# A row softmax with relative-position bias on one core: a gated second load, earlier scales, and counts ahead of two loops

## The chip, the core and the metric

The kernel runs on one core of a Trainium2 chip. The core has compute engines that run their own instruction streams: VectorE (DVE in the profile) and ScalarE (ACT) do the arithmetic here, GpSimd (POOL) only makes two small index tables, and SyncE (SP) does nothing but issue loads. Data moves between the chip's main memory (HBM) and the core's working memory through 16 DMA engines that serve several queues; here loads are issued by SP (queue q1) and stores by ScalarE (queue q10). Engines are ordered against each other by semaphores alone: an instruction can wait until a semaphore has a value and add to another when it ends.

The metric is the device time of one execution in microseconds (us), the median of several runs.

## The reference

```python
def reference(logits, rel_bias):          # logits (2, 8, 2112, 2112), rel_bias (8, 33), f32
    max_rel = 16
    pos = np.arange(S)
    rel = pos[:, None] - pos[None, :]
    rel_clipped = np.clip(rel, -max_rel, max_rel) + max_rel
    bias = rel_bias[:, rel_clipped].copy()
    logits = logits + bias[None, :, :, :]
    logits = logits - logits.max(axis=-1, keepdims=True)
    exp = np.exp(logits)
    return (exp / exp.sum(axis=-1, keepdims=True)).astype(np.float32)
```

There are 2 x 8 x 2112 = 33,792 rows of 2112 numbers. Each row gets a bias that depends only on the distance between row and column, clipped to 16 either way, and then a softmax. Input and output are 285.5 MB each.

## The kernel before

**Tiling.** Each of the 128 partitions owns 264 consecutive rows (`RP`) of one head. A chunk is 6 rows (`R`) of every partition, 128 x 6 x 2112 numbers, 6336 KB; it fills one of four buffers `X[0]` to `X[3]` (`NBUF`). Four chunks, 24 rows a partition (`G`), make one turn of the loops, and there are 11 turns (`K`), so 44 chunks.

**The bias.** Along a row the bias is a constant, then a band of 33 values around the diagonal, then a constant; from one row to the next it shifts by one column. At the start VectorE builds one long strip `F` of it in PSUM for all rows that a partition owns. That needs `rel_bias`, which ScalarE loads (line 120) into `F2` after VectorE has cleared the place (line 118). VectorE meanwhile makes small masks (lines 130 to 140), waits for the load (line 141), spreads the table over the partitions (line 142) and fills the strip (lines 145 to 167). At the start of each turn `window(k)` copies the 2135 columns (`SW`) that the next 24 rows need from `F` to `F2` (line 170), and `settle` waits until the copy has ended.

**The three loops.** They are written out by hand; no planner reorders them.

- SP issues the first four loads at once (lines 95 and 96). Then, for each later chunk, it waits until the store of the same buffer has landed (`st[m]`) and issues the load (lines 97 to 100).
- VectorE, for each chunk: `add(m)` waits for the load (`ld[m]`, line 181) and runs six instructions (line 184), one a row, each of which adds the bias, negates and takes the minimum over the row. `scale(m)` waits until all six exps are done (`expd`, line 207), takes six reciprocals of the sums in one instruction (line 208), announces them (`inv`) and scales rows 0 to 3 (line 211).
- ScalarE, for each chunk: `exps(m)` runs one exp a row, with the sum of the row as a by-product, as soon as that row's add is done (lines 190 to 198). `scale_rest(m)` scales rows 4 and 5 once `inv` says so (line 216). `store(k, m)` waits for six scaled rows (`scaled`, line 92) and issues the store (line 93).

`take(eng, sem, n)` (line 86) waits for a semaphore to reach n and takes n off it again; every wait of this kind has line 86 in the profile. `scales_begin` (line 200) is the wait on `inv` that both engines share.

Of the kernel before, what the change touches and what calls it, by code (L numbers as in the profile page):

```python
# [15 lines left out]
def kernel(  # L16
# [6 lines left out]
    nc = tc.nc  # L23
# [5 lines left out]
    RP = B * H * S // P  # L29
# [4 lines left out]
    NBUF = 4  # L34
    R = 6
    G = NBUF * R
    K = RP // G
    assert K * G == RP
    SW = S + G - 1
    DV = 4  # L40

    io = ctx.enter_context(tc.tile_pool(name="io", bufs=1))
    X = [io.tile([P, R * S], FP32, tag=f"X{b}", name=f"X{b}") for b in range(NBUF)]
    F2 = io.tile([P, SW + 1], FP32, tag="F2", name="F2")
# [4 lines left out]
    tot = io.tile([P, NBUF * R], FP32, tag="tot", name="tot")  # L49
    rec = io.tile([P, NBUF * R], FP32, tag="rec", name="rec")  # L50
    num = rec[:, 0 : NB + 1]
    ps = ctx.enter_context(tc.tile_pool(name="ps", bufs=1, space=bass.MemoryType.PSUM))
    F = ps.tile([P, 2560], FP32, tag="F", name="F")
# [11 lines left out]
    def view(t, offset, dims):  # L65
        return bass.AP(tensor=t.tensor, offset=t.offset + offset, ap=[[list(t.ap[0])[0], P]] + dims)

    def rows(t, k, m):
        return bass.AP(
            tensor=t.tensor, offset=t.offset + m * R * S + k * (G * S), ap=[[RP * S, P], [1, R * S]],  # L70
        )

    with tc.tile_critical(no_gpsimd_drain=True):  # L73
# [3 lines left out]
        expd = nc.alloc_semaphore("expd")  # L77
        scaled = nc.alloc_semaphore("scaled")
        inv = nc.alloc_semaphore("inv")
        rb = nc.alloc_semaphore("rb")  # L80
        zero = nc.alloc_semaphore("zero")
        idx = nc.alloc_semaphore("idx")
# [2 lines left out]
        def take(eng, sem, n):  # L85
            eng.wait_ge(sem, n).then_inc(sem, -n)  # L86

        def load(k, m):
            nc.sync.dma_start(out=X[m][:, :], in_=rows(logits, k, m)).then_inc(ld[m], 16)
# [2 lines left out]
            take(nc.scalar, scaled, R)  # L92
            nc.scalar.dma_start(out=rows(out, k, m), in_=X[m][:, :]).then_inc(st[m], 16)

        for m in range(NBUF):
            load(0, m)
        with nc.Fori(0, K - 1, 1, engines=[ENG.SP]) as k:
            for m in range(NBUF):
# [5 lines left out]
        v = nc.vector  # L104
        done = [0]

        def then(ins):
            done[0] += 1
            ins.then_inc(dve, 1)

        def settle():
            take(v, dve, done[0])
            done[0] = 0

        Q = 32
        step = list(F2.ap[0])[0]
        T = F2[:, 0 : H * W]
# [2 lines left out]
        nc.scalar.dma_start(  # L120
            out=bass.AP(tensor=F2.tensor, offset=F2.offset, ap=[[Q * step, P // Q], [1, H * W]]),
            in_=bass.AP(tensor=rel_bias.tensor, offset=rel_bias.offset, ap=[[0, P // Q], [1, H * W]]),
        ).then_inc(rb, 16)
        nc.gpsimd.iota(pid[:, :], pattern=[[0, 2]], base=0, channel_multiplier=1).then_inc(idx, 1)
        nc.gpsimd.iota(
            num, pattern=[[1, NB + 1]], base=0, channel_multiplier=0,
# [11 lines left out]
        for o, n, s, op in ((eq, NB, q, ALU.is_equal), (lt, NB, q, ALU.is_lt), (hsel, NB, h, ALU.is_equal),  # L138
                            (le, NB + 1, q, ALU.is_le), (gt, NB + 1, q, ALU.is_gt)):
            then(v.tensor_scalar(out=o, in0=num[:, 0:n], scalar1=s, scalar2=None, op0=op))  # L140
        v.wait_ge(rb, 16)
        then(v.stream_shuffle(out=T, in_=T, mask=[0] * Q))  # L142
        settle()
# [19 lines left out]
                           in_=view(reg, 1, [[1, NB - 1], [0, RP - W]])))  # L163
# [3 lines left out]
        settle()  # L167

        def window(k):
            then(v.tensor_copy(out=F2[:, 0:SW], in_=F[:, bass.ds(RP - G - k * G, SW)]))  # L170
            settle()

        def row(m, i):
            return X[m][:, i * S : (i + 1) * S]

        def col(t, m, i, n=1):
            c = m * R + i
            return t[:, c : c + n]
# [21 lines left out]
        def scales_begin(eng, m):  # L200
            if m < NBUF - 1:
                eng.wait_ge(inv, m + 1)
            else:
                take(eng, inv, NBUF)

        def scale(m):
            take(v, expd, R)
            v.reciprocal(out=col(rec, m, 0, R), in_=col(tot, m, 0, R)).then_inc(inv, 1 if m < NBUF - 1 else NBUF + 1)  # L208
            scales_begin(v, m)
            for i in range(DV):  # L210
                v.tensor_scalar_mul(out=row(m, i), in0=row(m, i), scalar1=col(rec, m, i)).then_inc(scaled, 1)  # L211

        def scale_rest(m):
            scales_begin(nc.scalar, m)
            for i in range(DV, R):
                nc.scalar.activation(  # L216
                    out=row(m, i), in_=row(m, i), func=ACTF.Copy, scale=col(rec, m, i),
                ).then_inc(scaled, 1)

        with nc.Fori(0, K, 1, engines=[ENG.DVE]) as k:  # L220
            window(k)
            for m in range(NBUF):
                add(m)
                scale(m)
        with nc.Fori(0, K, 1, engines=[ENG.Activation]) as k:
            for m in range(NBUF):
                exps(m)
                scale_rest(m)
                store(k, m)
# [31 lines left out]
```

## Time and profile before

| | |
|---|---|
| three runs | 1325.72, 1326.83 (the median), 1335.42 us |
| the profiled execution, its time | 1327.36 us |
| the profiled execution, its span | 1325.6 us |
| VectorE busy | 866.1 us |
| ScalarE busy | 757.2 us |
| bytes moved | 570.98 MB, mean 431 GB/s |
| 44 loads, 6336 KB each, issue to landing (median) | 39.0 us |
| 44 stores, 6336 KB each, issue to landing (median) | 58.8 us |

The span runs from the first to the last recorded instruction or transfer; the device time has a little around it. Busy times leave out instructions that only wait, branch or issue a DMA; their engine is then written DVEq, ACTq or SPq. In a group's row, the first pair of numbers is the busy time of the group in us and the mean of one in ns, and behind the second bar stands the time for which the engine sat idle just before these instructions, with what ended it. In a window's row come the stretch, its length, then for DVE, ACT and POOL the busy time and the instructions that started in it, the granted TensorE clock, the DMA engines' mean share and GB/s.

### The profile page before, as it was taken

What the parts mean: (1) busy time and instruction counts of PE and PEld (TensorE: products, weight loads), DVE (VectorE), ACT (ScalarE), POOL (GpSimd) and SP (SyncE); (2) the same over time, 40 slices, a digit from 0 to 9 for tenths busy, and PEclk for the clock granted to TensorE, in tenths of its full rate; (3) what the DMA queues carried; (4) which work ended last, traced back from release to release, by engine and by line L of the source; (5) the groups of instructions that cost most, each with busy time, mean ns of one, the idle gap of its engine ahead of it and who ended that gap; (6) DMA issues with size and microseconds to landing.
All of it is one profiled execution on the core that took longest, in us unless ns stands there. A gap on an engine that the chain in (4) does not pass through costs nothing. (4 is left out here: it accounts for less than half of the span.)

```text
span 1325.6 us, 2109 instructions
## 1 busy us (share of the span) xinstructions
DVE 866.1 (65%) x781; ACT 757.2 (57%) x627; POOL 0.4 (0%) x6
## 2 busy tenths in 40 slices
DVE  6886656566766675566667566556766676566663
ACT  3776555556665565555556565555665665555563
POOL 0000000000000000000000000000000000000000
DMA  9999999999999999999999999999999999999998
GB/s 416 416 433 424 441 428 428 441 424 433 441 428 431 436 425 433 439 430 434 434 430 433 437 434 425 437 434 434 428 439 436 422 441 434 431 431 436 428 433 389
DMA packets 12682, 570.98 MB, mean 431 GB/s; under 512 B 1412, under 2 KB 1416, under 8 KB 1416
## 3 DMA queue, kind: packets, MB, share of 16 engines
q1 hardware_dynamic: 6336, 285.48, 50.1%
q10 hardware_dynamic: 6344, 285.48, 49.8%
q14 instruction: 2, 0.02, 0.0%
HBM read 285.48 MB, written 285.47 MB: 431 GB/s over the span
## 5 line engine op out<-in xcount | busy, mean ns | idle before, releaser
L195 ACT ACTIVATE X<-X,nmax 128x2112 f32<-128x2112 f32 x264 | 542.6, 2055 | 508.0 <-DVE nmax L184 475.3
L184 DVE CUSTOM_DVE_ANT_0 X<-X,F 128x2112 f32<-128x2112 f32 x264 | 605.2, 2354 | 322.3 <-DVEq L86 322.3
L211 DVE TENSOR_SCALAR X<-X,rec 128x2112 f32<-128x2112 f32 x176 | 220.3, 1315 | 2.8
L216 ACT ACTIVATE X<-X,rec 128x2112 f32<-128x2112 f32 x88 | 176.1, 2048 | 17.2 <-DVE rec L208 12.2
L208 DVE RECIPROCAL rec<-tot 128x6 f32<-128x6 f32 x44 | 8.4, 191 | 106.2 <-DVEq L86 106.2
L195 ACT ACTIVATION_READ_ACCUMULATOR X<-X,nmax 128x1 f32 x264 | 49.2, 186 | 0.0
L195 ACT ACT_TABLE_LOAD x11 | 14.1, 1283 | 22.6 <-ACTq L86 19.9
L170 DVE COPY F<-F 128x2135 f32 x11 | 26.1, 2373 | 0.5 <-DVEq L86 0.5
L184 DVE DVE_READ_ACCUMULATOR2_ANT nmax<- 128x1 f32 x264 | 21.7, 82 | 0.0
L142 DVE LOAD_MASK_SELECT F<-F x1 | 0.0, 14 | 6.0 <-DMA F<-in_rel_bias_dram 6.0
L162 DVE COPY F<-own 128x1617 f32<-128x1617 f32 x1 | 1.8, 1835 | 0.0
L118 DVE MEMSET F<- 128x264 f32 x1 | 0.3, 278 | 1.1 <-SPq L73 1.1
L140 DVE TENSOR_SCALAR Z<-rec,Z 128x8 f32<-128x8 f32 (+1 forms) x5 | 0.8, 227 | 0.1
L148 DVE TENSOR_REDUCE own<-F 128x33 f32<-128x264 f32 x1 | 0.6, 608 | 0.1
L161 DVE TENSOR_TENSOR F<-F,own 128x264 f32<-128x264 f32 x1 | 0.4, 442 | 0.1
L145 DVE TENSOR_TENSOR F<-F,Z 128x264 f32<-128x264 f32 x1 | 0.4, 428 | 0.1
L142 DVE STREAM_SHUFFLE F<-F 128x264 f32<-128x264 f32 x1 | 0.4, 443 | 0.0
L158 DVE TENSOR_TENSOR F<-Z,own 128x264 f32<-128x264 f32 x1 | 0.4, 432 | 0.0
L166 DVE COPY F<-own 128x247 f32<-128x247 f32 x1 | 0.4, 410 | 0.0
L164 DVE COPY F<-own 128x247 f32<-128x247 f32 x1 | 0.4, 408 | 0.0
L156 DVE SCALAR_TENSOR_TENSOR own<-Z,own 128x8 f32<-128x8 f32 x1 | 0.2, 227 | 0.2 <-DVEq L86 0.2
L153 DVE TENSOR_SCALAR own<-Z,own 128x8 f32<-128x8 f32 x1 | 0.2, 226 | 0.1
(11 smaller groups left out, 1.6 us busy)
## 6 DMA issues: line engine op xcount, KB each, us to landing
X<-in_logits_dram SPq DMA_DIRECT2D x44, 6336.0 KB, 39.0
out_dram<-X ACTq DMA_DIRECT2D x44, 6336.0 KB, 58.8
F<-in_rel_bias_dram ACTq DMA_DIRECT2D x1, 4.1 KB
```

Source lines behind the costliest of these rows:

```text
L140: then(v.tensor_scalar(out=o, in0=num[:, 0:n], scalar1=s, scalar2=None, op0=op))
L142: then(v.stream_shuffle(out=T, in_=T, mask=[0] * Q))
L145: then(v.tensor_tensor(out=heads, in0=view(F2, 0, [[W, H], [1, W]]), in1=view(hsel, 0, [[1, H], [0, W]]), op=ALU.mult))
L148: then(v.tensor_reduce(out=rbK, in_=view(F2, H * W, [[1, W], [W, H]]), axis=mybir.AxisListType.X, op=ALU.add))
L158: then(v.tensor_tensor(out=bands, in0=view(eq, 0, [[1, NB], [0, W]]), in1=view(rbK, W - 1, [[0, NB], [-1, W]]), op=ALU.mult))
L162: then(v.tensor_copy(out=view(F, C0 + W, [[RP, NB - 1], [1, RP - W]]), in_=view(reg, 1, [[1, NB - 1], [0, RP - W]])))
L170: then(v.tensor_copy(out=F2[:, 0:SW], in_=F[:, bass.ds(RP - G - k * G, SW)]))
L184: v.tensor_tensor_reduce(out=row(m, i), in0=row(m, i), in1=F2[:, x : x + S], scale=-1.0, scalar=BIG, op0=ALU.add, op1=ALU.min, accum_out=c ...
L195: nc.scalar.activation(out=row(m, i), in_=row(m, i), func=ACTF.Exp, scale=-1.0, bias=col(nmax, m, i), accum_out=col(tot, m, i),).then_inc( ...
L208: v.reciprocal(out=col(rec, m, 0, R), in_=col(tot, m, 0, R)).then_inc(inv, 1 if m < NBUF - 1 else NBUF + 1)
L211: v.tensor_scalar_mul(out=row(m, i), in0=row(m, i), scalar1=col(rec, m, i)).then_inc(scaled, 1)
L216: nc.scalar.activation(out=row(m, i), in_=row(m, i), func=ACTF.Copy, scale=col(rec, m, i),).then_inc(scaled, 1)
```

## The change

Three things change.

- **The gate.** SP issues the load of the first chunk and then waits for a new semaphore `go`; the loads of chunks 2, 3 and 4 of the first turn follow after it. VectorE's `window(k)` copies the strip in two parts, 1100 columns (`C1`) and the remaining 1035, with a `settle` after each, and adds one to `go` between them. SP waits for it once only.
- **The scales.** `scale(m)` waits for four exps (`A`), takes four reciprocals, announces them and scales rows 0 to 2 (`D`) on VectorE; it then waits for the other two exps, takes their reciprocals, and scales rows 4 and 5. ScalarE scales row 3 alone. Before, VectorE had rows 0 to 3 and ScalarE rows 4 and 5.
- **The counts.** VectorE, after its masks and ahead of its wait for `rel_bias`, adds 1 to a semaphore 32 times and takes the 32 off again; ScalarE does the same 48 times after it has issued the load of `rel_bias`, ahead of its loop.

```diff
-    DV = 4
+    A, D = 4, 3
+    C1 = 1100
...
-        for m in range(NBUF):
+        load(0, 0)
+        nc.sync.wait_ge(go, 1)
+        for m in range(1, NBUF):
             load(0, m)
...
+        def fill(eng, sem, n):
+            for _ in range(n):
+                eng.sem_inc(sem, 1)
+            take(eng, sem, n)
...
+        fill(nc.scalar, padA, 48)
         nc.gpsimd.iota(pid[:, :], pattern=[[0, 2]], base=0, channel_multiplier=1).then_inc(idx, 1)
...
+        fill(v, padV, 32)
         v.wait_ge(rb, 16)
...
         def window(k):
-            then(v.tensor_copy(out=F2[:, 0:SW], in_=F[:, bass.ds(RP - G - k * G, SW)]))
+            x = RP - G - k * G
+            then(v.tensor_copy(out=F2[:, 0:C1], in_=F[:, bass.ds(x, C1)]))
+            settle()
+            v.sem_inc(go, 1)
+            then(v.tensor_copy(out=F2[:, C1:SW], in_=F[:, bass.ds(x + C1, SW - C1)]))
             settle()
...
         def scale(m):
-            take(v, expd, R)
-            v.reciprocal(out=col(rec, m, 0, R), in_=col(tot, m, 0, R)).then_inc(inv, 1 if m < NBUF - 1 else NBUF + 1)
+            def scales(first, stop):
+                for i in range(first, stop):
+                    v.tensor_scalar_mul(out=row(m, i), in0=row(m, i), scalar1=col(rec, m, i)).then_inc(scaled, 1)
+
+            take(v, expd, A)
+            v.reciprocal(out=col(rec, m, 0, A), in_=col(tot, m, 0, A)).then_inc(inv, 1 if m < NBUF - 1 else NBUF + 1)
             scales_begin(v, m)
-            for i in range(DV):
-                v.tensor_scalar_mul(out=row(m, i), in0=row(m, i), scalar1=col(rec, m, i)).then_inc(scaled, 1)
+            scales(0, D)
+            take(v, expd, R - A)
+            v.reciprocal(out=col(rec, m, A, R - A), in_=col(tot, m, A, R - A)).then_inc(invB, 1)
+            take(v, invB, 1)
+            scales(A, R)
 
         def scale_rest(m):
             scales_begin(nc.scalar, m)
-            for i in range(DV, R):
+            for i in range(D, A):
                 nc.scalar.activation(
```

More of the change, by code (lines that the diff above doesn't have):

```diff
@@ L79 @@
         inv = nc.alloc_semaphore("inv")
+        go = nc.alloc_semaphore("go")
+        padV = nc.alloc_semaphore("padV")
+        padA = nc.alloc_semaphore("padA")
+        invB = nc.alloc_semaphore("invB")
         rb = nc.alloc_semaphore("rb")
```

## The prediction

> **What bounds the kernel now.** I read the page from the top: busy shares of the engines first, then the 40 slices, then the DMA queues.
>
> ```profile
> span 1325.6 us, 2109 instructions
> DVE 866.1 (65%) x781; ACT 757.2 (57%) x627; POOL 0.4 (0%) x6
> DMA  9999999999999999999999999999999999999998
> DMA packets 12682, 570.98 MB, mean 431 GB/s; under 512 B 1412, under 2 KB 1416, under 8 KB 1416
> q1 hardware_dynamic: 6336, 285.48, 50.1%
> q10 hardware_dynamic: 6344, 285.48, 49.8%
> L184 DVE CUSTOM_DVE_ANT_0 X<-X,F 128x2112 f32<-128x2112 f32 x264 | 605.2, 2354 | 322.3 <-DVEq L86 322.3
> ```
>
> No compute engine is near full: VectorE idles a third of the span, 322.3 us of it at the wait for a load (line 86 called from `add`). The 16 DMA engines are at nine tenths or more in every slice but the last, and the load queue q1 and the store queue q10 together claim 50.1% + 49.8% = 99.9% of 16 engines' span. The kernel is a transfer of 570.98 MB with the arithmetic beside it. So the next view is the one that gives the rate by stretch, with the two ends finely cut. A row of X is 6 x 2112 x 4 = 50,688 bytes a partition; a DMA moves 128 of these, 8 for each of 16 engines. The window view counts a packet where it starts, so short windows show rounds of packets.
>
> ```profile
> 0.00:1.90 1.90, 0.59 (x4) 0.00 (x0) 0.43 (x6) 1.00 0.00 0
> 1.90:2.50 0.60, 0.52 (x4) 0.00 (x0) 0.00 (x0) 1.00 4.27 1352
> 17.00:17.60 0.60, 0.60 (x1) 0.00 (x0) 0.00 (x0) 1.00 0.00 0
> 17.60:18.20 0.60, 0.13 (x1) 0.00 (x0) 0.00 (x0) 1.00 3.13 1352
> 0.00:33.00 33.00, 22.87 (x35) 12.46 (x12) 0.43 (x6) 1.00 0.98 415
> 33.00:66.00 33.00, 28.66 (x27) 24.76 (x21) 0.00 (x0) 1.00 1.01 421
> 66.00:132.00 66.00, 49.99 (x45) 46.31 (x40) 0.00 (x0) 1.00 0.99 430
> 132.00:264.00 132.00, 82.63 (x73) 72.33 (x59) 0.00 (x0) 1.00 1.00 430
> 264.00:528.00 264.00, 175.22 (x155) 154.57 (x128) 0.00 (x0) 1.00 1.00 433
> 1056.00:1320.00 264.00, 164.53 (x147) 146.66 (x122) 0.00 (x0) 1.00 1.00 433
> 1322.00:1322.50 0.50, 0.00 (x0) 0.00 (x0) 0.00 (x0) 1.00 0.24 101
> 1322.50:1326.00 3.50, 0.00 (x0) 0.00 (x0) 0.00 (x0) 1.00 0.00 0
> ```
>
> The last two columns are the DMA share and GB/s. In 17.60:18.20, 1352 GB/s x 0.6 us = 811 KB, 16 packets: all 16 engines start their ninth packet, the first of chunk 2. Each costs 3.13 x 0.6 x 16 / 16 = 1.88 us. In 1.90:2.50 the very first 16 packets cost 4.27 x 0.6 = 2.56 us each, 0.68 more, because the engines start from rest. From 264 us on the rate is 433 GB/s and does not move.
>
> The span adds up from this alone: 570.98 MB / 433 GB/s = 1318.6 us; the slower rows lose 33 x (1 - 415/433) = 1.4, 33 x (1 - 421/433) = 0.9, 66 x 3/433 = 0.5 and 132 x 3/433 = 0.9, together 3.7; no packet starts after 1322.5, so some 3.3 us follow the last start. That is 1325.6. Only the 3.7 and the ends can be gained; only a hole in the DMA work can be lost.
>
> **The change, part by part.** *The scales.* Rows of chunk 1, from the timeline (start, duration):
>
> ```profile
> 27.90 2.06 ACT L195 ACTIVATE X<-X,nmax 128x2112 f32<-128x2112 f32 x1
> 32.35 0.08 DVE L184 DVE_READ_ACCUMULATOR2_ANT nmax<- 128x1 f32 x1
> 32.56 2.05 ACT L195 ACTIVATE X<-X,nmax 128x2112 f32<-128x2112 f32 x1 [0.23 <-ACTq L86]
> 34.85 0.19 DVE L208 RECIPROCAL rec<-tot 128x6 f32<-128x6 f32 x1 [2.43 <-DVEq L86]
> 35.08 5.01 DVE L211 TENSOR_SCALAR X<-X,rec 128x2112 f32<-128x2112 f32 x4
> 40.34 0.38 ACTq L93 DMA_DIRECT2D out_dram<-X  x1
> ```
>
> Today VectorE waits 2.43 us after its last add for the sixth exp, takes 0.23 to the first scale, and does four scales of 5.01/4 = 1.25. After: the fourth exp (27.90 + 2.06, and its accumulator read) is done near 30.2, before the adds end at 32.43, so that wait disappears. 32.43 + 0.1 + 0.23 = 32.76; three scales to 36.5; the sixth exp has long ended (34.8), a second reciprocal of 0.23; two scales to 39.2. ScalarE's one scale, 2.0 from 34.8, ends at 36.8. The store is issued near 39.4 instead of 40.34: 0.9 us sooner in each of 44 chunks. Is that on the path? The store then stands behind others:
>
> ```profile
> L93 ACTq DMA_DIRECT2D out_dram<-X x44: 338/338/380, 40.3 to 1306.3; - x44
> DMA to landing us min/median/max: 18.2/58.8/59.5
> 1303.00:1306.30 3.30, 3.05 (x3) 2.01 (x2) 0.00 (x0) 1.00 1.10 476
> 1306.30:1307.30 1.00, 0.00 (x0) 0.00 (x0) 0.00 (x0) 1.00 0.47 203
> 1307.30:1309.10 1.80, 0.00 (x0) 0.00 (x0) 0.00 (x0) 1.00 1.04 451
> ```
>
> A store takes 58.8 us (median) to land, though alone it lands in 18.2; some 40 us of queue and sharing cover it. Even the last one: around its issue at 1306.3 the engines are still moving the store before, 3.30 x 1.10 + 0.47 + 1.80 x 1.04 = 5.97 of 6.1 us. I cost the whole part at nothing; if the cover were gone, it would be worth 0.9 us at the end, once.
>
> *The counts.* 32 increments on VectorE and 48 on ScalarE, each set followed by a wait that resets it. Nothing like a bare increment loop is in the trace; the nearest rows are the wait-and-reset pairs and, from above, the hop between two dependent vector instructions.
>
> ```profile
> L86 DVEq EVENT_SEMAPHORE  x118: 21/21/21, 1.6 to 1300.9; - x118
> 9.33 0.43 DVE L145 TENSOR_TENSOR F<-F,Z 128x264 f32<-128x264 f32 x1
> 9.90 0.61 DVE L148 TENSOR_REDUCE own<-F 128x33 f32<-128x264 f32 x1
> 8.74 0.01 DVE L142 LOAD_MASK_SELECT F<-F  x1 [5.99 <-DMA F<-in_rel_bias_dram]
> 21.07 2.05 ACT L195 ACTIVATE X<-X,nmax 128x2112 f32<-128x2112 f32 x1 [17.10 <-DVE nmax L184]
> ```
>
> Lower end 0.021 us each, upper end 9.90 - 9.76 = 0.14. I take 0.06. VectorE: 32 x 0.06 = 1.9, at most 4.5, inside the 5.99 us in which it waits for rel_bias; it is uncovered only above 5.99/32 = 0.19 each. ScalarE: at most 48 x 0.14 = 6.7, inside 17.10. Cost nothing.
>
> *The gate.* SP (SyncE) issues chunk 1's load as before, then waits for `go`; behind that wait stand the loads of chunks 2 to 4 and SP's whole loop. `go` comes from VectorE when 1100 columns of the strip are copied.
>
> ```profile
> 12.38 1.83 DVE L162 COPY F<-own 128x1617 f32<-128x1617 f32 x1
> 14.44 0.41 DVE L166 COPY F<-own 128x247 f32<-128x247 f32 x1
> 15.35 2.38 DVE L170 COPY F<-F 128x2135 f32 x1 [0.50 <-DVEq L86]
> 18.66 2.36 DVE L184 CUSTOM_DVE_ANT_0 X<-X,F 128x2112 f32<-128x2112 f32 x1 [0.94 <-DVEq L86]
> 0.97 2.02 SPq L89 DMA_DIRECT2D X<-in_logits_dram  x4
> ```
>
> Copies cost (1.83 - 0.41)/(1617 - 247) = 1.04 ns a column and 0.15 us fixed, so 1100 columns take 1.30: 15.35 + 1.30 = 16.65. The hop 0.14, the increment 0.06 and SP's wake, about 0.1 (an estimate, between 0.02 and 0.14 as above): SP issues at about 16.95. From SP's first issue at 0.97 to the first packets at 1.90 to 2.50 passed 0.93 to 1.53, so chunk 2's packets start at 17.88 to 18.48, where before they started at 17.60 to 18.20: a hole of 0.3 us on all engines. Starting from rest, they may again pay the 0.68 of the first round. Sum +1.0. Ends: below, 0.0, if issuing is a little quicker and nothing starts from rest; above, the first part as dear as the whole copy (2.38), +1.1, so 2.1. I take 1.0, nearest to the one start from rest that the trace has.
>
> On the start, the Trainium skill (DMA: Bandwidth & Descriptors, section Latency and other measured facts) gives about 600 ns to the first byte for DMAs issued from SP; this trace shows 0.93 or more. By the page's figure the packets would come at 17.55, before the engines run dry, and the gate would cost nothing.
>
> The second copy (1035 columns, 0.15 + 1.08 = 1.2) ends near 18.2 with its register work, before chunk 1's load lets the first add go at 18.66, so it is hidden; in the ten later windows the extra 0.4 us stands before the wait for a load, where VectorE idles 322.3 us in all.
>
> **Sum.** 0 + 0 + 1.0: span 1326.6. The profiled execution took 1327.36, 1.8 around its span, and lies 0.5 above the median 1326.83. So 1328.4 for a profiled one and 1327.8 as the median.
>
> **The rivals.** *Gain in the loose stretches.* The 2.3 us lost between 33 and 264 us stand where stores begin to mix with loads. Shifted starts may mix better. For it: from 264 us on the same mix runs at 433. Against: nothing in the change orders those packets. With half of it and no price for the gate: 1326.8 - 1.2 = 1325.6; with all of it and the 1.0 paid: 1325.5. Nothing past that is to be had. The Trainium skill's DMA page (section Bandwidth) puts the ceiling of the ports at 435.2 GB/s; at that rate the bytes take 1312.0 us, an estimate that would give 1320 in all, still within 1% of before.
>
> *The counts are not covered,* the rival on the other side. Place: VectorE, ahead of the wait for rel_bias. It decides from 0.19 us a count; at 0.30, say because the instructions have to be fetched, `go` comes 32 x 0.30 - 6.0 = 3.6 later and every engine rests that long: 1331.4. To be slower by 1% it takes 12.3 us, 0.57 a count. Against it: every semaphore row here is far shorter.
>
> *The gate does nothing:* chunk 2's load reaches the engines before they run dry. It decides at 17.60 - 16.95 = 0.65 us from issue to first packet; the one row has 0.93, which speaks against it. 1326.8. (The Trainium skill's figure for the start, above, would bring it about.)
>
> *A run longer for no cause in the kernel:* one of the three times before is 1335.42.
>
> **How the numbers follow.** The forecast, a short hole of 0.3 to 2.1 us, has 0.55 (1327.1 to 1328.9); the gate without effect 0.15; the gain 0.15; counts uncovered 0.07; the long run 0.08. Range: floor 1324.0, below the gain's 1325.5 by the 1.1 that the lowest of the three times lies under the median and a little more; top 1332.0, over the 1331.4. Left out are the long run and the tails, under 2 in 10. Over 1% (13 us, about what a measurement of this kernel can tell from no change) faster would need more than all the losses: 0.01. Slower by that needs a hole twelve times my estimate: 0.04. Within: 0.95.
>
> **What would show it.** Right: DMA share unchanged at 99.9%; in the windows around 17.0 to 18.6 the ninth round starts some 0.3 later, at about 2.5 us a packet; the reciprocal's wait of 2.43 us gone and the stores' time to land longer by about what they are issued sooner; 433 GB/s after 264 us. Wrong: a hole of several us before the second load; ScalarE or VectorE waits that let the store queue run dry; a rate in the steady rows other than 433.

## The result, and the profile after

The changed kernel takes 1330.89 us (median of 22 executions, 1326.94 to 1334.69) against 1325.72 for the kernel before (median of 22, 1325.07 to 1337.29). The ratio is 1.0027, 95% interval 1.0014 to 1.0040: slower by a quarter of a per cent, clear of no change, inside the stated range. All 44 executions count in both; the ratio follows the means (1.0027), while the medians lie 0.4% apart, mostly because two executions of the kernel before are long (1335.42 and 1337.29). The profiled execution took 1330.56 with a span of 1328.8, 3.2 over that of before.

The page of the changed kernel, busy shares, queues, the groups that answer to those of before and the DMA issues (the last number is the median time to landing), then two rows from the windows:

```profile
span 1328.8 us, 2367 instructions
DVE 924.7 (70%) x880; ACT 666.8 (50%) x583; POOL 0.4 (0%) x6
DMA  9999999999999999999999999999999999999997
DMA packets 12683, 570.98 MB, mean 430 GB/s; under 512 B 1413, under 2 KB 1417, under 8 KB 1417
q1 hardware_dynamic: 6336, 285.48, 49.9%
q10 hardware_dynamic: 6344, 285.48, 49.6%
L202 DVE CUSTOM_DVE_ANT_0 X<-X,F 128x2112 f32<-128x2112 f32 x264 | 605.2, 2354 | 364.6 <-DVEq L91 364.6
L230 DVE RECIPROCAL rec<-tot 128x4 f32<-128x4 f32 x44 | 7.6, 172 | 0.0
X<-in_logits_dram SPq DMA_DIRECT2D x44, 6336.0 KB, 44.7
out_dram<-X ACTq DMA_DIRECT2D x44, 6336.0 KB, 54.0
264.00:528.00 264.00, 184.46 (x173) 135.69 (x119) 0.00 (x0) 1.00 1.00 433
1056.00:1320.00 264.00, 182.33 (x171) 133.76 (x117) 0.00 (x0) 1.00 0.98 426
```

The same bytes move, at 433 to 435 GB/s from 264 to 1056 us, where it was 433 before. One slice of the 40 is below nine tenths, the last, as before; it has 7 where it had 8, and the last window is down to 426 GB/s. The reciprocal waits for nothing now; VectorE's wait for loads has grown from 322.3 to 364.6 us, so the time that the new scale split saves is waited away again. Stores now land sooner (54.0 us instead of 58.8) and loads later (44.7 instead of 39.0). The loss is at the two ends. The start, from the timeline and from windows (last columns: DMA share, GB/s):

```profile
15.35 1.30 DVE L185 COPY F<-F 128x1100 f32 x1 [0.50 <-DVEq L91]
16.83 0.34 SPq L94 DMA_DIRECT2D X<-in_logits_dram  x1
17.00 1.24 DVE L188 COPY F<-F 128x1035 f32 x1 [0.34 <-DVEq L91]
...
17.00:17.60 0.60, 0.60 (x1) 0.00 (x0) 0.00 (x0) 1.00 0.00 0
17.60:18.20 0.60, 0.60 (x1) 0.00 (x0) 0.00 (x0) 1.00 2.67 845
18.20:18.80 0.60, 0.03 (x1) 0.00 (x0) 0.00 (x0) 1.00 0.91 338
18.80:20.00 1.20, 0.93 (x1) 0.00 (x0) 0.00 (x0) 1.00 0.31 84
```

The copy of 1100 columns ends at 16.65, SP issues at 16.83, and 845 x 0.6 = 507 KB, 10 packets instead of 16, start in 17.60:18.20. Four more follow in the next window and two after 18.80. They take 2.67 x 0.6 x 16 / 10 = 2.56 us each instead of 1.88. So the ninth round starts from rest and, unlike the first round, unevenly: over 1.8 us instead of 0.5.

The end, from the same two views:

```profile
1290.46 2.36 DVE L202 CUSTOM_DVE_ANT_0 X<-X,F 128x2112 f32<-128x2112 f32 x1 [9.48 <-DVEq L91]
...
1311.24 0.34 ACTq L98 DMA_DIRECT2D out_dram<-X  x1
...
1303.00:1306.30 3.30, 3.15 (x5) 3.08 (x3) 0.00 (x0) 1.00 0.71 307
1306.30:1307.30 1.00, 1.00 (x2) 1.00 (x3) 0.00 (x0) 1.00 0.23 101
1307.30:1309.10 1.80, 1.65 (x3) 1.14 (x1) 0.00 (x0) 1.00 0.20 84
1309.10:1311.90 2.80, 1.91 (x2) 0.00 (x0) 0.00 (x0) 1.00 0.04 18
1311.90:1312.40 0.50, 0.00 (x0) 0.00 (x0) 0.00 (x0) 1.00 3.81 1622
```

And the corresponding rows of the kernel before (its windows stand in the prediction):

```profile
1284.53 2.36 DVE L184 CUSTOM_DVE_ANT_0 X<-X,F 128x2112 f32<-128x2112 f32 x1 [8.49 <-DVEq L86]
...
1306.28 0.34 ACTq L93 DMA_DIRECT2D out_dram<-X  x1
```

Before, the DMA engines had work up to the last store. Now, between 1306.3 and 1311.9, they are nearly empty: they have moved nearly everything except the last chunk, and the last chunk is not ready. Its first add starts at 1290.46 instead of 1284.53, 5.9 us later, although its load was issued no later (at 1245.57, before at 1245.95). A load has landed when each of the 16 engines has moved its eight packets, and the trace records one 4-byte completion write for each engine. For the last load the first and the last of these 16 writes lie 2.1 us apart before and 8.7 us after. Some engines have fallen behind the others, and the last load waits for the slowest. The lag builds up along the run: in the changed kernel the same spread is 2.2 us for chunk 2, 5.6 for chunk 6, 7.0 for chunk 22 and 8.5 to 8.7 from chunk 27 on; in the kernel before it is 0.5 for chunk 2, 2.2 for chunk 6, and between 1.7 and 2.9 from there on.

The balance, from the trace's packet records (idle time as a mean over 16 engines): at the start 0.62 us after, 0.22 before, +0.4. At the end 5.38 after, 1.21 before, +4.2. The packets themselves, summed and divided by 16, 1321.4 after and 1322.7 before, -1.2. Within this the ninth round costs 0.6 more; against it stand fewer stretched packets (from 25 us on, 61 packets of the changed kernel's loads last over 0.1 us longer than the usual 1.87, and 166 of the kernel before). Together +3.4, against 3.3 between the ends of the last packets (1327.3 and 1324.0).

### The profile page after: what moved, and what is told of

It reads as the page before. It is cut to its first block, busy times and chain, and to the rows that moved or that the text cites. A ratio compares the mean times of both kernels' runs of the same rounds, so it can differ in the third digit from the quotient of the medians.

```text
span 1328.8 us, 2367 instructions
## 1 busy us (share of the span) xinstructions
DVE 924.7 (70%) x880; ACT 666.8 (50%) x583; POOL 0.4 (0%) x6
## 3 DMA queue, kind: packets, MB, share of 16 engines
q1 hardware_dynamic: 6336, 285.48, 49.9%
q10 hardware_dynamic: 6344, 285.48, 49.6%
## 5 line engine op out<-in xcount | busy, mean ns | idle before, releaser
L202 DVE CUSTOM_DVE_ANT_0 X<-X,F 128x2112 f32<-128x2112 f32 x264 | 605.2, 2354 | 364.6 <-DVEq L91 364.6
L227 DVE TENSOR_SCALAR X<-X,rec 128x2112 f32<-128x2112 f32 x220 | 278.4, 1316 | 9.4 <-DVEq L91 1.2
L241 ACT ACTIVATE X<-X,rec 128x2112 f32<-128x2112 f32 x44 | 89.7, 2039 | 0.0
L188 DVE COPY F<-F 128x1035 f32 x11 | 13.6, 1236 | 3.7 <-DVEq L91 3.7
L185 DVE COPY F<-F 128x1100 f32 x11 | 14.3, 1296 | 0.5 <-DVEq L91 0.5
L230 DVE RECIPROCAL rec<-tot 128x4 f32<-128x4 f32 x44 | 7.6, 172 | 0.0
L234 DVE RECIPROCAL rec<-tot 128x2 f32<-128x2 f32 x44 | 6.9, 158 | 0.0
## 6 DMA issues: line engine op xcount, KB each, us to landing
X<-in_logits_dram SPq DMA_DIRECT2D x44, 6336.0 KB, 44.7
```

The source lines that it names most:

```text
L185: then(v.tensor_copy(out=F2[:, 0:C1], in_=F[:, bass.ds(x, C1)]))
L188: then(v.tensor_copy(out=F2[:, C1:SW], in_=F[:, bass.ds(x + C1, SW - C1)]))
L202: v.tensor_tensor_reduce(out=row(m, i), in0=row(m, i), in1=F2[:, x : x + S], scale=-1.0, scalar=BIG, op0=ALU.add, op1=ALU.min, accum_out=c ...
L230: v.reciprocal(out=col(rec, m, 0, A), in_=col(tot, m, 0, A)).then_inc(inv, 1 if m < NBUF - 1 else NBUF + 1)
L234: v.reciprocal(out=col(rec, m, A, R - A), in_=col(tot, m, A, R - A)).then_inc(invB, 1)
L241: nc.scalar.activation(out=row(m, i), in_=row(m, i), func=ACTF.Copy, scale=col(rec, m, i),).then_inc(scaled, 1)
```

## The experiments

Theory 1: the gate makes the engines start chunk 2 from rest and unevenly; they stay apart, and the last load lands late. Rivals: the earlier scales shift stores against loads (2); the gate costs its hole alone (3).

**One part at a time.** `gate_only` is before with the gate and the split copy:

```diff
+    C1 = 1100
...
-        for m in range(NBUF):
+        load(0, 0)
+        nc.sync.wait_ge(go, 1)
+        for m in range(1, NBUF):
             load(0, m)
...
```

> The kernel before with the gate and the split strip copy alone. Theory 1 (the gate makes the 16 DMA engines start chunk 2 from rest and unevenly; they stay out of step, the last load lands late on the slowest of them, and the last store with it): as slow as the changed kernel, about 1330 us, 4 to 5 over before, the last store issued near 1310. Theory 2 (the earlier scales shift stores against loads and cause it): about 1326.5, last store near 1306. Theory 3 (the gate costs its hole alone): 1326.5 to 1327, last store near 1307.

`scales_only` is before with the new `scale` and `scale_rest` alone:

```diff
-    DV = 4
+    A, D = 4, 3
...
```

> The kernel before with the new scale split alone. Theory 1: no more than 0.5 us from before (1325.7), the last store issued about 0.9 us sooner, near 1305.4. Theory 2: about 1330 us.

`counts_only` is before with the two `fill` calls alone:

```diff
...
+        fill(nc.scalar, padA, 48)
...
+        fill(v, padV, 32)
...
```

> The kernel before with the 32 and 48 counts alone. All theories: 1325.7, within 0.5 us, because the counts end before VectorE's wait for rel_bias and ScalarE's first exp. If the counts shift the engines' phase, several us.

`no_gate` is the changed kernel without the wait:

```diff
-        nc.sync.wait_ge(go, 1)
```

> The changed kernel without SP's wait; the strip copy is still split and go is still counted up. Theory 1: back to 1325.7, within 0.5 us. Theory 2: still about 1330. Theory 3: some 1 us below the changed kernel, about 1329.5.

On this chip the kernel before itself spread more: median 1329.46 of 35 executions, 16 of them below 1327 and 12 above 1334. Beside it: `gate_only` median 1332.62 (ratio 1.0022, 0.9999 to 1.0045), `scales_only` 1336.04 (1.0016, 0.9986 to 1.0046), `counts_only` 1336.08 (1.0029, 1.0001 to 1.0057), `no_gate` 1327.71 (0.9992, 0.9962 to 1.0021).

So `no_gate` is level with the kernel before, where the changed kernel was slower in its own set. That speaks for theory 1 and against 2 and 3, but it is not clear of noise: the intervals of the two ratios overlap, and that of `gate_only` just includes 1. Theory 1 also said that scales alone and counts alone would stay within 0.5 us, and that did not come: 1 and 0 of their 12 executions were below 1327, though only the ratio of `counts_only` is clear of 1, and barely. Their profiled executions (1336.21 and 1335.85) show the same hole before the last store, without any gate. Windows of `counts_only`, then of `scales_only`:

```profile
1303.00:1306.30 3.30, 3.10 (x4) 2.96 (x5) 0.00 (x0) 1.00 0.71 307
1306.30:1314.90 8.60, 5.20 (x5) 6.07 (x4) 0.00 (x0) 1.00 0.15 65
1314.90:1316.00 1.10, 0.00 (x0) 0.00 (x0) 0.00 (x0) 1.00 1.63 691
```

```profile
1303.00:1306.30 3.30, 3.30 (x5) 3.04 (x5) 0.00 (x0) 1.00 0.61 261
1306.30:1315.80 9.50, 8.19 (x9) 5.70 (x5) 0.00 (x0) 1.00 0.12 53
1315.80:1317.00 1.20, 0.00 (x0) 0.00 (x0) 0.00 (x0) 1.00 1.59 676
```

In both, 0.12 to 0.15 of the engines' time is used for some 9 us. In `no_gate` the store is ready in time:

```profile
1304.42 0.34 ACTq L98 DMA_DIRECT2D out_dram<-X  x1
...
1303.00:1306.30 3.30, 1.20 (x1) 0.00 (x0) 0.00 (x0) 1.00 0.90 384
1306.30:1309.10 2.80, 0.00 (x0) 0.00 (x0) 0.00 (x0) 1.00 0.84 362
```

The hole before the last store is how a long execution comes about in these profiles; the gate is at most one way to it, not the only one.

**Is it the two queues?** Theory 4: an engine may get ahead on loads and behind on stores, because it alternates between two queues. `one_queue` issues the stores from SP too, in a fixed order:

```diff
-            nc.scalar.dma_start(out=rows(out, k, m), in_=X[m][:, :]).then_inc(st[m], 16)
+            nc.sync.dma_start(out=rows(out, k, m), in_=X[m][:, :]).then_inc(st[m], 16)
...
+            for m in range(NBUF):
+                store(k, m)
+                p = (m - 1) % NBUF
+                take(nc.sync, st[p], 16)
+                load(k + 1 if m > 0 else k, p)
...
```

> The kernel before with loads and stores both issued by SP on one queue, in a fixed order (store of chunk c, then the load of chunk c+3), so that every DMA engine works through the same list. Theory 4 (the DMA engines get out of step between the load queue and the store queue during the run; a load then lands late on the engine that is behind, the last store is issued late, and the other engines run dry before it): the landings of one DMA stay within about 1 us over the 16 engines up to the end, no executions above 1330, all near 1324.5. Theory 5 (the times above 1330 come from the memory or the chip and not from the two queues): the times spread from 1325 to 1337 as those of the kernel before.

`one_queue_gate` adds the gate and the split copy to it.

> The same with the gate and the split strip copy. Theory 4: the gate costs its own hole alone, 0.4 to 1.0 us over the kernel with one queue and no gate. If the gate costs 4 us or more here too, it is not by the two queues that its unevenness is kept.

Beside these, the kernel before had a median of 1326.70 (35 executions, 18 below 1327). `one_queue` took 1331.21 (1329.24 to 1333.06; ratio 1.0017, 0.9994 to 1.0039), `one_queue_gate` 1330.49 (1.0013, 0.9990 to 1.0035). Theory 4 fell as an account of where the lag comes from: with one list for every engine the completion writes of one DMA still drift apart, from 0.5 us for chunk 2 to 9.8 late in the run. Sorting the packet records of `one_queue` into 16 chains, one behind the other, gives eleven that end near 1322.5 and five that end between 1325.4 and 1329.3; five of the chains have about twenty stretched packets each, some 6 to 11 us in sum, the other eleven 1 to 4, and 1 to 2 us. The sorting goes by times alone, since the records don't name the engine, and where two engines run at the same time it may swap them; so it is not shown that the five with the stretched packets are the five that end late. The gate added nothing here: the hole at the start (0.59 us idle against 0.15) is there, but the median is 0.7 lower. Neither kernel has an execution below 1327 or above 1334, so with one queue both the long and the short executions of the kernel before are missing.

**Is it the late store alone?** `fine_tail` is the changed kernel with its last chunk done row by row and stored in three pieces:

```diff
+        for j in range(0, R, 2):
+            nc.sync.wait_ge(fin, j + 2)
+            nc.sync.dma_start(
...
+        for i in range(R):
+            add_row(z, i)
+            if i > 1:
+                one_scale(i - 2)
...
```

> The changed kernel, gate and all, with its last chunk done row by row (scale i after add i+2) and stored in three pieces of two rows from SP, the first some 8 us sooner than the whole store. Theory 4: the engines get as far out of step as in the changed kernel, but the hole before the last store goes: 4 to 6 us below the changed kernel, 1325 to 1326, with little spread. If the engines' skew costs its time before the tail: no gain, about 1330.

No gain: 1331.93 (1327.50 to 1334.72). Timeline and windows of its end:

```profile
1291.97 2.36 DVE L216 CUSTOM_DVE_ANT_0 X<-X,F 128x2112 f32<-128x2112 f32 x1 [9.55 <-DVEq L92]
...
1304.29 11.05 SPq L111 DMA_DIRECT2D out_dram<-X  x3
...
1313.50:1323.00 9.50, 1.33 (x2) 0.00 (x0) 0.00 (x0) 1.00 0.97 411
1323.00:1329.00 6.00, 0.00 (x0) 0.00 (x0) 0.00 (x0) 1.00 0.18 76
```

The first piece is issued 12.3 us after the chunk's first add, instead of the 20.8 of the changed kernel, and the engines are busy again to 1323. But in the next 6 us 0.18 of their time is still used, up to 1328.9: the engines that lag finish late themselves, whenever the store is issued. My expectation had this as its second case. The hole before the last store and the late end are two sides of one lag.

**Is it the start from rest?** `gate_early` is the changed kernel with a shorter first copy:

```diff
-    C1 = 1100
+    C1 = 100
```

> The changed kernel with 100 columns in place of 1100: SP issues chunk 2's load about 1 us sooner, near 15.9, so that its packets are queued before chunk 1's run out. Theory 1 (it is the start from rest): the ninth round starts with chunk 1's last packets at 17.6, within 0.5 us, and the times are those of the kernel without the gate. If the wait itself matters and not the rest: as the changed kernel, 1330.

It took 1330.09 (1326.58 to 1339.84), ratio 1.0027 (1.0003 to 1.0050), like the changed kernel, but it did not do what it was made for. The load was issued 1 us sooner, at 15.83, and the engines went to rest all the same:

```profile
15.83 1.29 SPq L94 DMA_DIRECT2D X<-in_logits_dram  x3
...
17.50:18.10 0.60, 0.60 (x1) 0.00 (x0) 0.00 (x0) 1.00 0.96 352
18.10:18.70 0.60, 0.17 (x1) 0.00 (x0) 0.00 (x0) 1.00 1.64 507
18.70:19.40 0.70, 0.09 (x1) 0.00 (x0) 0.00 (x0) 1.00 1.40 434
```

Packets begin from 17.9 to 19.4, 2.1 to 3.6 us after the issue. So two more kernels move the gate further, one each way. `gate_at_9` opens the gate far ahead, `gate_rest` far behind:

```diff
         then(v.stream_shuffle(out=T, in_=T, mask=[0] * Q))
         settle()
+        v.sem_inc(go, 1)
...
             settle()
-            v.sem_inc(go, 1)
```

> The changed kernel with go counted up right after the shuffle of rel_bias, near 9.2 us, instead of between the two copies; SP waits as before. Chunk 2's load is then issued some 8 us before chunk 1's packets run out. Theory 1 (the uneven start from rest): the ninth round starts at 17.6 to 18.2 with packets of 1.88 us, chunk 2's landings lie within 0.5 to 1.3 us, and the times are those of the kernel without the gate in this call. If the gate costs its time by the wait itself: as the changed kernel in this call.

```diff
             settle()
-            v.sem_inc(go, 1)
...
             take(v, ld[m], 16)
+            if m == 0:
+                v.sem_inc(go, 1)
```

> The changed kernel with go counted up after chunk 1 has landed, near 18.9 us: all 16 engines are at rest for some 2 us and start chunk 2 together, as they started chunk 1. Theory 1a (what matters is that some engines start sooner than others, 17.8 to 19.6 in the changed kernel): starts within 0.6 us, landings of chunk 2 within 1 us, and the time is that of the kernel without the gate plus the hole of 2 to 2.7 us. Theory 1b (any start from rest sets the engines apart): as the changed kernel plus 1.5 to 2 us more of hole.

Beside them, on the same chip, the changed kernel and the one without the gate once more:

> The changed kernel once more, on the same chip and beside the others of this call: 1327 to 1332 as in its first 22 executions.

> The changed kernel without SP's wait once more, beside the changed kernel on one chip: most executions at 1325.7 to 1328, some near 1336. Theory 1: median 3 to 5 us below the changed kernel.

Beside these four, the kernel before took 1327.08 (28 executions, 13 below 1327). `after_again` took 1332.38 (ratio 1.0037, 1.0017 to 1.0057) and `no_gate_again` 1328.03 (1.0011, 0.9986 to 1.0035): again the kernel without the gate is the faster, by 4.3 us between the medians, though the two intervals overlap. `gate_rest` took 1335.87 (7 executions; 1.0051, 1.0020 to 1.0081) and `gate_at_9` 1332.87 (1.0037, 1.0015 to 1.0058). Windows of `gate_rest`, then of `gate_at_9`:

```profile
18.20:20.20 2.00, 0.85 (x2) 0.00 (x0) 0.00 (x0) 1.00 0.00 0
20.20:21.00 0.80, 0.80 (x1) 0.00 (x0) 0.00 (x0) 1.00 3.06 1014
```

```profile
17.50:18.10 0.60, 0.60 (x1) 0.00 (x0) 0.00 (x0) 1.00 2.35 1014
18.10:18.70 0.60, 0.28 (x1) 0.00 (x0) 0.00 (x0) 1.00 0.78 338
```

In `gate_rest` all 16 engines start chunk 2 within 0.8 us (1014 x 0.8 = 811 KB, 16 packets) after a rest, and its completion writes lie 0.7 us apart. In `gate_at_9` nothing rests at all: 12 + 4 packets follow on chunk 1 as before. Both end with the last load's writes 9.0 to 9.5 us apart. So an even start does not protect, and theory 1 in the form "the uneven start is the cause" fell too. The other form, that any start from rest sets the engines apart, cannot account for `gate_at_9`, where nothing rested.

All in one table. Its rows come from four sets of runs, on more than one chip, so medians compare within a set: first the two kernels themselves, then the next four rows (kernel before 1329.46), the next four (1326.70) and the last four (1327.08). Spreads are of the 16 completion writes, in the profiled execution; for the kernels with one queue the last DMA is a store.

| kernel | spread, chunk 2 | spread, last load | last issue of a store | profiled, us | median, us (n) | below 1327 |
|---|---|---|---|---|---|---|
| before | 0.5 | 2.1 | 1306.3 | 1327.36 | 1325.72 (22) | 19 |
| changed | 2.2 | 8.7 | 1311.2 | 1330.56 | 1330.89 (22) | 1 |
| gate_only | 1.9 | 12.9 | 1316.6 | 1335.88 | 1332.62 (12) | 0 |
| scales_only | 0.8 | 7.7 | 1315.0 | 1336.21 | 1336.04 (12) | 1 |
| counts_only | 1.4 | 5.4 | 1314.1 | 1335.85 | 1336.08 (12) | 0 |
| no_gate | 1.3 | 3.5 | 1304.4 | 1325.77 | 1327.71 (12) | 5 |
| one_queue | 0.5 | (6.8) | 1306.6 | 1333.05 | 1331.21 (12) | 0 |
| one_queue_gate | 1.7 | (6.4) | 1303.9 | 1330.38 | 1330.49 (12) | 0 |
| fine_tail | 2.2 | 10.0 | 1315.0 | 1332.14 | 1331.93 (12) | 0 |
| gate_early | 1.5 | 7.1 | 1311.6 | 1331.05 | 1330.09 (12) | 1 |
| gate_at_9 | 0.9 | 9.0 | 1310.7 | 1331.90 | 1332.87 (12) | 1 |
| gate_rest | 0.7 | 9.5 | 1316.6 | 1335.87 | 1335.87 (7) | 0 |
| changed, again | 2.5 | 11.4 | 1314.0 | 1333.51 | 1332.38 (10) | 1 |
| no_gate, again | 1.2 | 2.6 | 1303.7 | 1326.84 | 1328.03 (12) | 5 |

In the eleven rows that keep two queues and the whole last store, the profiled time follows the last store's issue: 19.3 to 23.1 us after it, whatever the edit. The two columns of spread don't follow each other: 0.5 at the start goes with 2.1 at the end, 0.7 to 0.9 with 7.7 to 9.5.

## Why the prediction was right, and where its account was not

*What bounds the kernel:* right. From 264 to 528 us the engines move 433 GB/s in the changed kernel as in the kernel before (432 to 434 in every other kernel here), and the loss is at the ends.

*The counts:* right in size. ScalarE's table load moved from 2.68 to 6.25 with 48 counts, 0.074 us each where I took 0.06, and VectorE's 32 vanish in a wait that is still 5.99. That they cost nothing in the end is not shown: `counts_only` ran slower than before on its chip (ratio 1.0029, its interval just clear of 1), with DMA engines out of step.

*The scales:* the working was right. From the last chunk's first add to its store's issue it is 20.78 us instead of 21.75, 0.97 sooner where I said 0.9.

*The gate:* the hole was sized well. The issue came at 16.83 (I said 16.95), with 0.4 us of rest more than before and 0.6 for packets from rest, 1.0 as forecast. What it did not have is the unevenness: packets start from 17.82 to 19.58, where it said 17.88 to 18.48. The Trainium skill (DMA: Bandwidth & Descriptors, section Latency and other measured facts) has about 600 ns to the first byte; the trace does not agree, with 1.0 us from the issue to the first packet and 2.75 until the last of the 16 engines had its first.

*The step that failed* is in the part on the scales, and the gate's price rests on it: "I cost the whole part at nothing", because "the engines are still moving the store before". The sum 0 + 0 + 1.0 therefore has no term for the end, and the changed kernel pays 4.2 us there. The reading behind it was wrong to begin with. The 5.97 of 6.1 us count the last store's own packets too: the packet records have them from 1307.13 on, 0.85 us after the issue, and fifteen of the sixteen engines have started theirs by 1308.3. So once the last store could start, the store before held an engine for 0 to 2 us longer, and that is all the cover there was. And even this cover is one of the profiled execution: it holds only while the 16 engines are in step. A load counts as landed when the slowest of 16 engines is done, so in the changed kernel the last chunk starts 5.9 us late by their lag, and the cover is gone. The Trainium skill (DMA: Bandwidth & Descriptors, section Why a DMA increments its semaphore by 16 and not by 1) says as much of landing: each engine that takes part writes its own increment after its data, and only the full count means landed. The trace agrees: 8.7 us between the first and the last of the 16 writes.

*The signs* named ahead: the ninth round at about 2.5 us a packet, the reciprocal's wait gone and 433 GB/s after 264 us all came. The queues' share did not stay at 99.9% (49.9% + 49.6% = 99.5%), and the stores' time to land became 4.8 us shorter, not 0.9 longer. One sign of being wrong came true, at the end: VectorE's wait for the last load let the store queue run dry.

The direction and the range held, and of the cases that I listed the likeliest came true at the start of the kernel. But the measured 3.2 to 5.2 us (spans, medians) are three to five times the forecast 1.0, and most of them lie at the other end. That the range holds 1330.89 is luck: the forecast case ends at 1328.9, and the range reaches to 1332.0 only because of the counts left uncovered, 1331.4, which did not happen. The rival "a run longer for no cause in the kernel" is probably the same mechanism unseen: the kernel before has long executions too, 2 of 22, 12 of 35, 8 of 35 and 4 of 28 above 1334 in the four sets. None of those was profiled, so that they come about in the same way is likely and not shown.

*What stays open:* why the engines drift apart. The numbers of short executions point to the gate, without showing how it acts: over all sets, the two-queue kernels with a gate and the whole last store have 4 of 75 executions below 1327, the changed kernel without it 10 of 24, the kernel before 66 of 120. But scales alone and counts alone, without a gate, have 1 of 24. Neither the uneven start, nor the rest, nor the two queues explains it, since kernels without each of these drift as far; in the profiled executions scales alone and counts alone drift, and the two together without a gate do not. Stretched packets go with the drift, by 0.1 to 1.5 us each; with two queues nearly all of these are loads, while stores keep their 1.87. Their number does not decide it: the kernel before, which stays nearest to step, has 166 of them, the changed kernel 61. Sorted into chains by time as above, the 166 fall on all sixteen, 7 to 15 each; of the 61 about eleven chains have 3 or fewer and four or five have 6 to 12. So what counts seems to be how evenly they fall. What stretches them was not tried.

No kernel here beats the one before; `no_gate` equals it (0.9992, 0.9962 to 1.0021).

## What to carry to other kernels

When a kernel is bound by DMA, add up its two ends apart from its middle, and ask how many microseconds of other transfers still cover the last dependent chain; if that is no more than the spread between the DMA engines, an edit anywhere near the start may show up at the end. One profile shows one draw of that spread: compare many executions, and look at the whole distribution, before a quarter of a per cent is put down to an edit.

## What the runs showed of the hardware that was not expected

- Sixteen DMA engines with equal lists did not stay in step; the completion writes of one DMA spread from 0.5 us at the start to 2.1 at the end in one execution, to 12.9 in another, and with one queue for everything to 9.8.
- The time from issue to the first packet was 1.0 us for the first load of every kernel, and 0.85 for the last store of the kernel before. The sixteen engines' first packets of the second load began 1.0 to 1.7 us after the issue in `gate_rest`, 1.0 to 2.75 in the changed kernel, and 2.1 to 3.6 in `gate_early`, issued 1.0 us sooner; the first store of the kernel before took 4.5 (issued at 40.34, first packet at 44.8). What sets this was not tried.
- Counting up ahead of a loop moved the fetch of code: the packet records have 8 KB instruction transfers at 40.1 and 87.9 us in the kernel before and at 12.1 and 15.7 in the changed one; at 10.2 and 18.1 with the counts alone, at 39.6 and 87.0 with the gate alone. Whether this bears on the drift was not tried.
